# Gates of half the tokens through an accumulated table in DRAM

## The chip, the cores and the metric

The kernel runs on one core of a Trainium2 chip. A core has TensorE (matrix products into PSUM), VectorE, ScalarE and GpSimd (called POOL in the profile), SyncE, which here only issues DMAs, and 16 DMA engines that all queues share. The metric is the device time of one execution in microseconds; "span" is the part of it between the first and the last recorded instruction.

## The reference

A two-layer encoder for 256 tokens of width 1024. Layer 0 mixes tokens by a short gated convolution, layer 1 by windowed attention. After each mixer comes the part that this change is about, an expert layer with 8 heads (PEER). For each token and head it scores 128 + 128 sub-keys, takes the best 16 of each, adds them in pairs, keeps the best 16 of the sums as expert numbers out of 128 x 128, and weighs these with a softmax, the gates:

```python
top_v, pos = lax.top_k(cand, PEER_TOPK)
idx = jnp.take_along_axis(cidx, pos, axis=-1)
g = jax.nn.softmax(top_v, axis=-1)
...
h = jnp.einsum("cd,ced->ce", xc, u)
a = gc.astype(xc.dtype) * jax.nn.gelu(h, approximate=False)
return jnp.einsum("ce,ced->cd", a, jnp.take(v_tab, ic, axis=0))
```

So a token's output is a sum over its 128 selected experts. One expert can be selected by several heads of a token; its gates then add up.

## The kernel before

The kernel doesn't gather experts. It computes all 16384 of them for every token and multiplies by a dense matrix of gates that is zero where an expert was not selected. Everything is done in float32 split in two float32r parts, so each weight tile of 128 x 1024 is loaded by SyncE (`raw`), copied to `hi` by ScalarE (L171) and reduced to `lo` by VectorE (L172). `take()` hands out the tiles in a fixed order, loaded some tiles ahead.

One expert layer (`peer`, L597) runs in these stages, named by the PSUM tiles that TensorE writes:

- `pq` and `psc`: 16 query tiles and the scores of the sub-keys. The sub-keys (1 MB) come by a DMA on POOL's queue (L600).
- `ph`, twice 64 expert columns j (two halves): `hm[i, j, t]` is the GELU of token t with expert i*128 + j, where i is the partition. 64 KB per partition and half.
- `pv`: 128 rows j. `split_pair(j)` (L805) splits two rows of `hm` (ScalarE, then VectorE) into a ring that lies in the memory of `xn`, and twelve products of 512 columns per row accumulate into four banks.

The selection runs on VectorE beside these stages. `Background` (L35) holds a list of steps, each with a planned cost; every query tile, expert column and row calls `pump()`, which issues as many steps as the plan allows: `plan(cost, calls)` spreads `cost` over `calls`. The steps are `side` (best 16 of 128 sub-keys), `candidates`, `pick` (best 16 sums), `decode`, `lookup` and `total` (expert numbers), `gates` (softmax), `turned` (three products that put tokens on the free axis), and, ahead of ph, `normed`, which makes `xn`, the input of ph, out of `xr`.

When half 0 of ph is done, `one_hots` and `spread` build the dense gates of that half, eight tokens at a time: VectorE compares an iota with i (L754) and with j (L756), multiplies the second by three bfloat16 parts of the gate (L758), TensorE multiplies the two for each token (three products of 64 columns, PSUM tile `pg`), and VectorE multiplies the 128 x 64 result of eight tokens into `hm` (L770). These steps are spread over half 1 of ph; those of half 1 over the first rows of pv.

What sets the order: the engines each work in the order in which the program emits instructions for them, `tc.issue_after(x)` emits after x, and the framework adds waits for data and for buffers. POOL's queue carries, in this order, the write of the bias rows (L443) in the convolution, the sub-keys, the bias loads for attention (L449, L451) in the second half of pv of layer 0, the sub-keys of layer 1, and one load at the end (L858).

Of the kernel before, what the change touches and what calls it, by code (L numbers as in the profile page):

```python
# [17 lines left out]
P = 128  # L18
T = 256
# [11 lines left out]
NEG = -1e30  # L31
ROUTE, SPREAD, WARM = 88.0, 2.6, (9, 2, 2, 2, 4, 2)

# [38 lines left out]
def trunk_kernel(  # L72
# [77 lines left out]
    G.iota(iota2, pattern=[[1, P], [0, 2]], base=0, channel_multiplier=0, allow_small_or_imprecise_dtypes=True)  # L150
    i1T = const.tile([P, T], BF16, name="i1T")
    i2T = const.tile([P, T], BF16, name="i2T")
    gT = const.tile([P, 3, T], BF16, name="gT")
# [4 lines left out]
    zeros = const.tile([P, 512], BF16, name="zeros")  # L158
    V.memset(zeros, 0.0)
    S.activation(stat[:, 10:11], eps, AF.Square)  # L160
    squares = const.tile([P, 512], BF16, name="squares")

# [99 lines left out]

    def squares_of(t, h):
        return S.activation(
            squares, xs[:, t, 512 * h : 512 * h + 512], AF.Square, accum_out=stat[:, 2 * t + h : 2 * t + h + 1]
        ).ins
# [122 lines left out]
    def conv_mixer(sc):  # L389
# [35 lines left out]
        for k in range(KC - 2):  # L425
            rows_product(acc, take(), z[:, k, :T], z[:, k, T:], k == 0)
        return last_rows(acc, [(take(KC - k), z[:, k, :T], z[:, k, T:]) for k in (KC - 2, KC - 1)])


# [167 lines left out]
    def peer(layer, last, meanwhile):  # L597
# [44 lines left out]

        def candidates(t):
            s = sv[:, t].rearrange("p (h s) k -> p h s k", s=2)
            a, b = s[:, :, 0], s[:, :, 1]
            V.tensor_tensor(
                cand[:, :, 0:2].rearrange("p h r c -> p h (r c)"), b, a[:, :, 0:1].to_broadcast([P, PH, TOPK]), ALU.add
            )
            V.tensor_tensor(
                cand[:, :, 2:9],  # L650
                a[:, :, 1:8, None].to_broadcast([P, PH, 7, 8]),
                b[:, :, None, 0:8].to_broadcast([P, PH, 7, 8]),
                ALU.add,
            )
            V.tensor_tensor(cand[:, :, 9], a[:, :, 8:16], b[:, :, 0:1].to_broadcast([P, PH, 8]), ALU.add)
# [4 lines left out]
        def decode(t):  # L660
            flat = tp.rearrange("p h k -> p (h k)")
            V.tensor_scalar(line, flat, 3, None, op0=ALU.logical_shift_right)
            V.tensor_scalar(col, flat, 7, None, op0=ALU.bitwise_and)
            V.tensor_copy(linef, line)
            V.tensor_copy(colf, col)
            V.scalar_tensor_tensor(beyond, linef, 9.0, colf, op0=ALU.is_equal, op1=ALU.mult)
            V.tensor_tensor(colf, colf, beyond, ALU.subtract)
            V.scalar_tensor_tensor(ab[:, 0], linef, -1.0, beyond, op0=ALU.add, op1=ALU.add)
            V.tensor_scalar(ab[:, 0], ab[:, 0], 0.0, None, op0=ALU.max)
            V.tensor_scalar(linef, linef, 1.0, 8.0, op0=ALU.is_equal, op1=ALU.mult)  # L670
            V.tensor_tensor(ab[:, 1], linef, colf, ALU.add)

        def lookup(t, s):

            if s == 0:
                V.tensor_copy(sib, si[:, t, :, :, None].to_broadcast([P, NSUB, TOPK, 2]))
            V.tensor_tensor(
                pick16.rearrange("p a (k d) -> p a k d", d=2),
                ab[:, s, None, :].to_broadcast([P, TOPK, P]).rearrange("p a (k d) -> p a k d", d=2),
                iota16[:, :, None, :].to_broadcast([P, TOPK, P // 2, 2]),  # L680
                ALU.is_equal,
            )
            ids = sib.rearrange("p (h s) a d -> p s h a d", s=2)[:, s]
            for h in range(PH):
# [3 lines left out]
        def total(t, s):  # L688
            for n in (8, 4, 2):
                V.tensor_tensor(pick16[:, 0:n], pick16[:, 0:n], pick16[:, n : 2 * n], ALU.add)  # L690
            V.tensor_tensor(sel[:, s], pick16[:, 0], pick16[:, 1], ALU.add)

        def gates(t):
            g = sel[:, 2].rearrange("p (h k) -> p h k", h=PH)
            V.tensor_tensor(g, tv, tv[:, :, 0:1].to_broadcast([P, PH, TOPK]), ALU.subtract)
            S.activation(g, g, AF.Exp)
            V.tensor_reduce(small[:, 0], g, axis=AX.X, op=ALU.add)
            V.reciprocal(small[:, 1], small[:, 0])
            V.tensor_tensor(g, g, small[:, 1, :, None].to_broadcast([P, PH, TOPK]), ALU.mult)

        def turned(t):
# [3 lines left out]
            c = slice(P * t, P * t + P)  # L705
            S.copy(i1T[:, c], b[:, 0])
            S.copy(i2T[:, c], b[:, 1])
            r = beyond
            V.tensor_copy(gT[:, 0, c], b[:, 2])
            V.tensor_tensor(r, b[:, 2], gT[:, 0, c], ALU.subtract)  # L710
            V.tensor_copy(gT[:, 1, c], r)
            V.tensor_tensor(gT[:, 2, c], r, gT[:, 1, c], ALU.subtract)

        bg.plan(ROUTE, NSUB + HALF - 4)
        for c4 in range(0, NSUB, 4):
            q = qT[(c4 // 4) % 2]
            for c in range(c4, c4 + 4, 2):
                b = bank("u", "pq")
                for i in range(2):
                    cols_product(b[:, T * i : T * i + T], take(), xr, c + i)  # L720
                    bg.pump()
                S.copy(q[:, c - c4 : c - c4 + 2], b.rearrange("p (a t) -> p a t", a=2))
            if c4 == 0:
                factors()
                for k in range(0, KC, 2):
                    bg.add(2.2, normed, k)
# [7 lines left out]
        for t in range(NT):  # L734
            bg.add(0.9, candidates, t)
            for h in range(PH):
                bg.add(0.9, pick, t, h)
            bg.add(1.7, decode, t)
            for s in range(2):
                bg.add(3.4, lookup, t, s)  # L740
                bg.add(1.3, total, t, s)
            bg.add(0.7, gates, t)
            bg.add(0.6, turned, t)

# [15 lines left out]
        def spread(hm, t0, made):  # L760
            oh1, oh2 = made.pop(t0)
            b = bank("g", "pg").rearrange("p (t i) -> p t i", t=8)
            for t in range(8):
                for j in range(3):
# [3 lines left out]
                    )  # L768
            c = slice(t0, t0 + 8)
            V.tensor_tensor(hm[:, :, c], b.rearrange("p t i -> p i t"), hm[:, :, c], ALU.mult)  # L770
# [3 lines left out]
        for half in range(2):  # L774
# [28 lines left out]
        acc = accumulators("pv")  # L803

        def split_pair(j):  # L805
            a = aring[:, (j // 2) % 4]
            src = halves[j // HALF][:, j % HALF : j % HALF + 2].rearrange("p a t -> p (a t)")
            S.copy(a[:, 0], src)  # L808
            V.tensor_tensor(a[:, 1], src, a[:, 0].bitcast(F32), ALU.subtract)  # L809


        kept, held = (2, 3)[layer], []
        split_pair(0)
        for j in range(0, P, 2):
            if j == HALF - 2:
# [3 lines left out]
            if j + 2 < P:  # L819
                split_pair(j + 2)  # L820
            a = aring[:, (j // 2) % 4]
# [24 lines left out]

    last = peer(0, last, prepare_attention)
    last = attention(held.pop(), last)

# [123 lines left out]
```

## Time and profile before

| | |
|---|---|
| Median of 3 runs | 1840.79 us (1840.71 to 1844.92) |
| The profiled execution | 1841.05 us, span 1839.1 us |
| TensorE busy | 1821.1 us (99%), granted clock 0.999 |
| VectorE busy | 1459.1 us (79%) |
| ScalarE busy | 918.3 us (50%) |
| POOL busy | 10.8 us (1%), 20 instructions |
| Moved by DMA | 322.62 MB, mean 175 GB/s |

How to read the profile: a group of instructions stands on one line with its source line, engine, operation, the tile it writes and the tiles it reads, the shape, the count, then busy time in all and the mean of one in ns, then the idle time of the engine just before them and what ended it. The chain is the work that ended last, followed back from the end; in order of time its rows have start, duration and the instruction. In windows each engine has its busy time within a stretch.

### The profile page before, as it was taken

Reading aid. Unit: us, or ns where it says so; the run is one execution under the profiler, and the core shown is the slowest. Engines: PE = TensorE matmul, PEld = TensorE weight load, DVE = VectorE, ACT = ScalarE, POOL = GpSimd, SP = SyncE. Lnnn points to the kernel's source line nnn. Section 1 sums busy time; section 2 is a strip of 40 time slices with the busy share of each in tenths; the row PEclk is TensorE's granted clock in tenths of the full one; section 3 lists DMA queues with packets and bytes.
Section 4 is the critical chain, followed back from the end, with each engine's and each line's share of the span. In section 5 each row is a group of like instructions: output and inputs, shape, how many; then the busy total and the mean of one; then the engine's idle time right before and its main releaser. Section 6 shows DMA issues by size and latency. Waiting matters only on the chain.

```text
span 1839.1 us, 33102 instructions
## 1 busy us (share of the span) xinstructions
PE 1821.1 (99%) x13007; PEld 1598.9 (87%) x13007; DVE 1459.1 (79%) x2917; ACT 918.3 (50%) x1236; POOL 10.8 (1%) x20
## 2 busy tenths in 40 slices
PE   9999999999999999999999999999999999999998
PEld 7999999988888888888887999999888888888886
DVE  7868988688888898655575789877888899885555
ACT  5465455544454443444475655555445544444444
POOL 0000000000000001000000000000000000000000
PEclk9999999999999999999999999999999999999999
DMA  6654555555555556656643555555555555555553
GB/s 209 195 183 161 184 184 183 173 166 167 172 162 182 162 168 201 227 191 196 193 131 102 171 164 184 184 183 172 173 163 161 181 162 169 164 185 194 194 194 126
DMA packets 89047, 322.62 MB, mean 175 GB/s; under 512 B 10235, under 2 KB 10428, under 8 KB 88636
## 3 DMA queue, kind: packets, MB, share of 16 engines
q1 hardware_dynamic: 87120, 314.61, 53.7%
q0 software_dynamic: 1392, 5.81, 0.9%
q8 instruction: 101, 1.65, 0.4%
q14 instruction: 54, 0.44, 0.1%
q10 hardware_dynamic: 380, 0.10, 0.0%
HBM read 319.40 MB, written 1.08 MB: 174 GB/s over the span
## 4 chain that ended last, share of the span: by engine, by line
PE 96%; DVE 2%; ACT 1%; DMA 0%; issue 0%; ACTq 0%; DVEq 0%
PE ph L107 39%; PE pv L107 37%; PE pq L107 6%; PE pg L107 5%; PE pconv L107 2%; PE pwo L107 1%; PE psc L107 1%; PE pout L107 1%; PE pgate L107 1%; PE po L107 0%; DVE lo L172 0%; PE pk L107 0%; PE ptr L111 0%; PE pwarm L107 0%; DMA mix<-in_sink 0%; ACT xn L301 0%
## 5 line engine op out<-in xcount | busy, mean ns | idle before, releaser
L172 DVE TENSOR_TENSOR lo<-raw,hi 128x1024 fp32r<-128x1024 f32 (+1 forms) x597 | 726.2, 1219 | 257.0 <-ACT hi L171 142.7
L171 ACT CAST hi<-raw 128x1024 fp32r<-128x1024 f32 (+1 forms) x597 | 625.5, 1049 | 535.2 <-PE ph L107 214.3
L107 PE MATMUL ph<-xn,hi 128*128 128x512 f32 (+1 forms) x2592 | 515.8, 347 | 0.0
L107 PE MATMUL pv<-hi,xn 128*128 128x512 f32 x2048 | 509.2, 389 | 0.0
L107 PEld LDWEIGHTS pv<-hi,xn 128*128 128x128 f32 x2048 | 384.4, 188 | 81.1
L107 PEld LDWEIGHTS ph<-xn,hi 128*128 128x128 f32 x2592 | 403.2, 190 | 48.4
L107 PEld LDWEIGHTS ph<-xn,lo 128*128 128x128 f32 x2048 | 273.2, 191 | 16.0 <-DVE lo L172 1.3
L107 PE MATMUL ph<-xn,lo 128*128 128x256 f32 x2048 | 281.9, 283 | 0.9 <-DVE lo L172 0.9
L107 PE MATMUL pv<-lo,xn 128*128 128x512 f32 x1024 | 279.8, 393 | 0.4 <-DVE lo L172 0.4
L107 PEld LDWEIGHTS pv<-lo,xn 128*128 128x128 f32 x1024 | 189.6, 188 | 38.3 <-DVE lo L172 1.1
L808 ACT CAST xn<-hm 128x512 fp32r<-128x512 f32 x128 | 79.0, 623 | 190.2 <-PE pv L107 187.7
L758 DVE TENSOR_TENSOR oh<-oh,gT 128x512 bf16<-128x512 bf16 x384 | 139.1, 417 | 0.0
L809 DVE TENSOR_TENSOR xn<-hm,xn 128x512 fp32r<-128x512 f32 x128 | 87.6, 689 | 61.4 <-ACT xn L808 61.4
L107 PEld LDWEIGHTS <-oh 128*128 128x128 bf16 x3072 | 96.2, 97 | 9.7 <-issue 8.4
L107 PE MATMUL pg<-oh,oh 128*128 128x64 bf16 x3072 | 103.9, 193 | 0.0
L788 ACT ACTIVATE hm<-hm 128x512 f32<-128x512 f32 x94 | 59.4, 632 | 85.7 <-DVE hm L227 85.7
L754 DVE TENSOR_TENSOR oh<-iota,i1T 128x1024 bf16<-128x1024 bf16 x128 | 87.5, 684 | 12.0 <-PE pg L107 12.0
L770 DVE TENSOR_TENSOR hm<-pg,hm 128x512 f32<-128x512 f32 x128 | 87.3, 684 | 1.8 <-PE pg L107 1.7
L107 PE MATMUL pq<-xr,hi 128*128 128x256 f32 x512 | 68.7, 285 | 0.3
L107 PEld LDWEIGHTS pq<-xr,hi 128*128 128x128 f32 x512 | 64.4, 192 | 2.1 <-ACT xr L301 1.7
L227 DVE TENSOR_TENSOR hm<-ph,hm 128x512 f32<-128x512 f32 x94 | 64.1, 682 | 0.0
L226 ACT COPY hm<-ph 128x512 f32<-128x512 f32 x94 | 54.7, 582 | 0.0
(170 smaller groups left out, 1051.2 us busy)
## 6 DMA issues: line engine op xcount, KB each, us to landing
raw<-in_u SPq DMA_DIRECT2D x256, 512.0 KB, 3.6
raw<-in_v SPq DMA_DIRECT2D x256, 512.0 KB, 3.4
raw<-in_w_q SPq DMA_DIRECT2D x32, 512.0 KB, 3.4
raw<-in_w_in SPq DMA_DIRECT2D x23, 512.0 KB, 3.8
raw<-in_w_qk SPq DMA_DIRECT2D x10, 512.0 KB, 3.4
raw<-in_w_out SPq DMA_DIRECT2D x8, 512.0 KB, 3.4
raw<-in_w_o SPq DMA_DIRECT2D x8, 512.0 KB, 3.4
mix<-bias_dram POOLq DMA_DIRECT2D x8, 384.0 KB, 10.5
```

The costliest lines, as they stand in the source:

```text
L107: newest[:] = [PE.matmul(*a, **k).ins]
L171: S.copy(hi[:, c], raw[:, c])
L172: bg.behind = V.tensor_tensor(lo[:, c], raw[:, c], hi[:, c].bitcast(F32), ALU.subtract).ins
L226: S.copy(dst, b[:, :, T:])
L227: V.tensor_tensor(dst, b[:, :, :T], dst, ALU.add)
L754: V.tensor_tensor(oh1, iota2[:, None].to_broadcast([P, 4, P, 2]), pairs(i1T, P), ALU.is_equal)
L758: V.tensor_tensor(oh2[:, 1 + j], oh2[:, 0], pairs(gT[:, j], HALF), ALU.mult)
L770: V.tensor_tensor(hm[:, :, c], b.rearrange("p t i -> p i t"), hm[:, :, c], ALU.mult)
L788: S.activation(hm[:, j : j + 2], hm[:, j : j + 2], AF.Gelu)
L808: S.copy(a[:, 0], src)
L809: V.tensor_tensor(a[:, 1], src, a[:, 0].bitcast(F32), ALU.subtract)
```

## The change

For the first 128 tokens the dense gates are no longer made from one-hots. They are added up in a table in DRAM, `table[i, j*128 + t]`, 128 x 16384 float32 (8.4 MB):

- `blank_table(n)` writes zeros into it with eight 1 MB DMAs on POOL's queue, n of them in flight: in layer 0 in the third column of the convolution, in layer 1 ahead of attention.
- `sent` works out on VectorE, for each token (partition) and each of its 128 selections, the address (i*128 + j)*128 + t, and `scatter(h)` issues for each head 16 indirect DMAs with addition, one for each of the 16 selections, each with one address and one gate per partition. The first two DMAs of a head wait until all of the head before have landed, since two heads can name the same cell.
- In pv, `load_gates(j)` loads two rows' gates for all first tokens (128 partitions x 1 KB), in a ring of two buffers on POOL's queue, and `gated(j)` multiplies them into `hm` on VectorE ahead of `split_pair(j)`.
- The second 128 tokens go by one-hots as before; those steps, `i1T`, `i2T`, `gT` and the transposes are there for 128 tokens only.
- The selection steps take a range of heads. Of token half 0, heads 0 and 1 are done first, during the query tiles and ahead of `normed`; then heads 2 to 7 of it, then token half 1. Planned costs change; `normed` is emitted at the latest at the end of the query tiles.

```diff
-ROUTE, SPREAD, WARM = 88.0, 2.6, (9, 2, 2, 2, 4, 2)
+FIRST, SPREAD, WARM = 24.0, 2.6, (9, 2, 2, 2, 4, 2)
...
             if j == 2:
                 bias_rows(sc)
+                blank_table(1)
...
+    table = dram.tile([P, P * P], F32, name="table")
+    cells = table.rearrange("p (f o) -> (p f) o", o=1)
+    ROWS = 2048
...
+    def blank_table(n):
+
+        blanked[:] = [bg.behind] * n
+        for i in range(P * P // ROWS):
+            dst = table[:, ROWS * i : ROWS * i + ROWS].rearrange("p (a c) -> p a c", c=256)
+            ins = nc.gpsimd.dma_start(dst, blank[:, None, :].to_broadcast([P, ROWS // 256, 256])).ins
+            wait_for(ins, blanked[:1])
+            blanked[:] = blanked[1:] + [ins]
+
+    def scatter(h):
+
+        earlier = blanked[:] if h == 0 else group[:]
+        group.clear()
+        for k in range(TOPK):
+            c = slice(TOPK * h + k, TOPK * h + k + 1)
+
+            def one():
+                group.append(
+                    nc.gpsimd.indirect_dma_start(
+                        cells, bass.IndirectOffsetOnAxis(ap=place[:, c], axis=0), gate[:, c], None,
+                        compute_op=ALU.add,
+                    ).ins
+                )
+
+            if k < 2:
+                one()
+                wait_for(group[k], earlier)
+            else:
+                with tc.issue_after(group[0]):
+                    one()
+            for g in group[:-1]:
+                tc.declare_no_dep(group[-1], g, reason="other cells")
...
+        def sent(h0, h1):
+
+            c = slice(TOPK * h0, TOPK * h1)
+            V.scalar_tensor_tensor(linef[:, c], sel[:, 0, c], float(P), sel[:, 1, c], op0=ALU.mult, op1=ALU.add)
+            V.tensor_scalar(place[:, c], linef[:, c], float(P), token, op0=ALU.mult, op1=ALU.add)
+            for h in range(h0, h1):
+                scatter(h)
...
+        def routed(t, h0, h1):
+            n = (h1 - h0) / PH
+            bg.add(0.3 + 0.6 * n, candidates, t, h0, h1)
+            for h in range(h0, h1):
+                bg.add(1.0, pick, t, h)
+            bg.add(1.2 + 1.3 * n, decode, t, h0, h1)
+            for s in range(2):
+                bg.add(0.4 + 3.2 * n, lookup, t, s, h0, h1)
+                bg.add(0.5 + 0.9 * n, total, t, s, h0, h1)
+            bg.add(0.5 + 0.4 * n, gates, t, h0, h1)
+            if t == 0:
+                bg.add(0.4, sent, h0, h1)
+            else:
+                bg.add(1.0, turned)
...
-        bg.plan(ROUTE, NSUB + HALF - 4)
+        bg.plan(FIRST, NSUB)
...
-                for c in range(c4, c4 + 4):
-                    bg.add(1.0, side, t, c)
...
+            for c in range(c4, c4 + 4):
+                bg.add(1.4, side, 0, c)
+            if c4 == 0:
+                routed(0, 0, 2)
+                for k in range(0, KC, 2):
+                    bg.add(2.2, normed, k)
+                last_normed = bg.steps[-1]
+        while last_normed in bg.steps:
+            bg.step()
+        routed(0, 2, PH)
+        for c in range(NSUB):
+            bg.add(1.4, side, 1, c)
+        routed(1, 0, PH)
+        bg.plan(sum(step[0] for step in bg.steps), HALF - 4)
...
-            bg.plan(SPREAD * T // 8, HALF - 4)
+            bg.plan(SPREAD * P // 8, HALF - 4)
             made = {}
-            for t0 in range(0, T + 8, 8):
-                if t0 < T:
+            for t0 in range(0, P + 8, 8):
+                if t0 < P:
                     bg.add(SPREAD - 0.6, one_hots, half, t0, made)
...
+        ended = bg.behind
...
+        first, gates_of, sent_last = [], {}, group[:]
+
+        def load_gates(j):
+            g = strm.tile([P, 2, P], F32, tag="gates", name="gates", bufs=2)
+            load = lambda: nc.gpsimd.dma_start(g, table[:, P * j : P * j + 2 * P].rearrange("p (a t) -> p a t", a=2)).ins
+            if not first:
+                first.append(load())
+                wait_for(first[0], sent_last)
+            else:
+                with tc.issue_after(first[0]):
+                    load()
+            gates_of[j] = g
+
+        def gated(j, behind):
+            h = halves[j // HALF][:, j % HALF : j % HALF + 2, :P]
+            with tc.issue_after(behind):
+                return V.tensor_tensor(h, h, gates_of.pop(j), ALU.mult).ins
...
         kept, held = (2, 3)[layer], []
+        load_gates(0)
+        load_gates(2)
+        ins = gated(0, ended)
+        load_gates(4)
         split_pair(0)
+        gated(2, ins)
+        load_gates(6)
         for j in range(0, P, 2):
...
             if j + 2 < P:
-                split_pair(j + 2)
+                ins = split_pair(j + 2)
+            if j + 4 < P:
+                gated(j + 4, ins)
+            if j + 8 < P:
+                load_gates(j + 8)
...
     last = peer(0, last, prepare_attention)
+    blank_table(2)
     last = attention(held.pop(), last)
```

More of the change, by code (lines that the diff above doesn't have):

```diff
@@ L150, in trunk_kernel @@
     G.iota(iota2, pattern=[[1, P], [0, 2]], base=0, channel_multiplier=0, allow_small_or_imprecise_dtypes=True)
-    i1T = const.tile([P, T], BF16, name="i1T")
-    i2T = const.tile([P, T], BF16, name="i2T")
-    gT = const.tile([P, 3, T], BF16, name="gT")
+    token = const.tile([P, 1], F32, name="token")
+    G.iota(token, pattern=[[0, 1]], base=0, channel_multiplier=1, allow_small_or_imprecise_dtypes=True)
+    i1T = const.tile([P, P], BF16, name="i1T")
+    i2T = const.tile([P, P], BF16, name="i2T")
+    gT = const.tile([P, 3, P], BF16, name="gT")
+    place = const.tile([P, P], U32, name="place")
+    gate = const.tile([P, P], F32, name="gate")
     stat = const.tile([P, 16], F32, name="stat")
@@ L157, in trunk_kernel @@
     V.memset(eps, EPS * D)
-    zeros = const.tile([P, 512], BF16, name="zeros")
-    V.memset(zeros, 0.0)
+    blank = const.tile([P, 256], F32, name="blank")
+    V.memset(blank, 0.0)
+    zeros = blank.bitcast(BF16)
     S.activation(stat[:, 10:11], eps, AF.Square)
-    squares = const.tile([P, 512], BF16, name="squares")
     def split_tile(src, spare=False, pieces=1):
@@ L263, in squares_of @@
     def squares_of(t, h):
+        squares = strm.tile([P, 512], BF16, tag="gates", name="squares", bufs=2)
         return S.activation(
@@ L427, in conv_mixer, with wait_for @@
         return last_rows(acc, [(take(KC - k), z[:, k, :T], z[:, k, T:]) for k in (KC - 2, KC - 1)])
+    table = dram.tile([P, P * P], F32, name="table")
+    cells = table.rearrange("p (f o) -> (p f) o", o=1)
+    ROWS = 2048
+    blanked, group = [], []
+    def wait_for(ins, others):
+        for o in others:
+            tc.add_manual_dep(
+                ins, o.name, mybir.DependencyInfo(mybir.DependencyClass.Sync, mybir.DependencyReason.DATA),
+                reason="transfers of one table in turn",
+            )
[17 more added lines that the diff above has]
+                    ).ins
+                )
+            if k < 2:
[6 more added lines that the diff above has]
+                tc.declare_no_dep(group[-1], g, reason="other cells")
     bias_dram = dram.tile([HEADS, 511], F32, name="bias_dram")
@@ L639, in side, with candidates @@
             best16(sv[:, t, c], si[:, t, c], scores[:, t, c], rest[turn[0] % 4])
-        def candidates(t):
-            s = sv[:, t].rearrange("p (h s) k -> p h s k", s=2)
+        def candidates(t, h0, h1):
+            n = h1 - h0
+            s = sv[:, t, 2 * h0 : 2 * h1].rearrange("p (h s) k -> p h s k", s=2)
             a, b = s[:, :, 0], s[:, :, 1]
+            to = cand[:, h0:h1]
             V.tensor_tensor(
-                cand[:, :, 0:2].rearrange("p h r c -> p h (r c)"), b, a[:, :, 0:1].to_broadcast([P, PH, TOPK]), ALU.add
+                to[:, :, 0:2].rearrange("p h r c -> p h (r c)"), b, a[:, :, 0:1].to_broadcast([P, n, TOPK]), ALU.add
@@ L648, in candidates @@
             )
             V.tensor_tensor(
-                cand[:, :, 2:9],
-                a[:, :, 1:8, None].to_broadcast([P, PH, 7, 8]),
-                b[:, :, None, 0:8].to_broadcast([P, PH, 7, 8]),
+                to[:, :, 2:9],
+                a[:, :, 1:8, None].to_broadcast([P, n, 7, 8]),
+                b[:, :, None, 0:8].to_broadcast([P, n, 7, 8]),
                 ALU.add,
             )
-            V.tensor_tensor(cand[:, :, 9], a[:, :, 8:16], b[:, :, 0:1].to_broadcast([P, PH, 8]), ALU.add)
+            V.tensor_tensor(to[:, :, 9], a[:, :, 8:16], b[:, :, 0:1].to_broadcast([P, n, 8]), ALU.add)
@@ L657, in pick @@
         def pick(t, h):
             best16(tv[:, h], tp[:, h], cand[:, h].rearrange("p r c -> p (r c)"), crest[h % 2])
[L660 to L671, printed above, removed]
@@ L673, in lookup, with decode @@
-        def lookup(t, s):
+        def decode(t, h0, h1):
+            c = slice(TOPK * h0, TOPK * h1)
+            flat = tp[:, h0:h1].rearrange("p h k -> p (h k)")
+            r, o, rf, of, by = (a[:, c] for a in (line, col, linef, colf, beyond))
+            V.tensor_scalar(r, flat, 3, None, op0=ALU.logical_shift_right)
+            V.tensor_scalar(o, flat, 7, None, op0=ALU.bitwise_and)
+            V.tensor_copy(rf, r)
+            V.tensor_copy(of, o)
+            V.scalar_tensor_tensor(by, rf, 9.0, of, op0=ALU.is_equal, op1=ALU.mult)
+            V.tensor_tensor(of, of, by, ALU.subtract)
+            V.scalar_tensor_tensor(ab[:, 0, c], rf, -1.0, by, op0=ALU.add, op1=ALU.add)
+            V.tensor_scalar(ab[:, 0, c], ab[:, 0, c], 0.0, None, op0=ALU.max)
+            V.tensor_scalar(rf, rf, 1.0, 8.0, op0=ALU.is_equal, op1=ALU.mult)
+            V.tensor_tensor(ab[:, 1, c], rf, of, ALU.add)
@@ L675, in lookup @@
+        def lookup(t, s, h0, h1):
+            n, c = TOPK * (h1 - h0), slice(TOPK * h0, TOPK * h1)
             if s == 0:
-                V.tensor_copy(sib, si[:, t, :, :, None].to_broadcast([P, NSUB, TOPK, 2]))
+                V.tensor_copy(
+                    sib[:, 2 * h0 : 2 * h1], si[:, t, 2 * h0 : 2 * h1, :, None].to_broadcast([P, 2 * (h1 - h0), TOPK, 2])
+                )
             V.tensor_tensor(
-                pick16.rearrange("p a (k d) -> p a k d", d=2),
-                ab[:, s, None, :].to_broadcast([P, TOPK, P]).rearrange("p a (k d) -> p a k d", d=2),
@@ L680, in lookup @@
-                iota16[:, :, None, :].to_broadcast([P, TOPK, P // 2, 2]),
+                pick16[:, :, c].rearrange("p a (k d) -> p a k d", d=2),
+                ab[:, s, None, c].to_broadcast([P, TOPK, n]).rearrange("p a (k d) -> p a k d", d=2),
+                iota16[:, :, None, :].to_broadcast([P, TOPK, n // 2, 2]),
                 ALU.is_equal,
@@ L683, in lookup, with total, gates, turned @@
             ids = sib.rearrange("p (h s) a d -> p s h a d", s=2)[:, s]
-            for h in range(PH):
+            for h in range(h0, h1):
                 e = pick16[:, :, TOPK * h : TOPK * h + TOPK].rearrange("p a (k d) -> p a k d", d=2)
                 V.tensor_tensor(e, e, ids[:, h, :, None, :].to_broadcast([P, TOPK, TOPK // 2, 2]), ALU.mult)
-        def total(t, s):
+        def total(t, s, h0, h1):
+            c = slice(TOPK * h0, TOPK * h1)
             for n in (8, 4, 2):
[L690 to L695, printed above, removed]
-            S.activation(g, g, AF.Exp)
[L697 to L701, printed above, removed]
+                V.tensor_tensor(pick16[:, 0:n, c], pick16[:, 0:n, c], pick16[:, n : 2 * n, c], ALU.add)
+            V.tensor_tensor(sel[:, s, c], pick16[:, 0, c], pick16[:, 1, c], ALU.add)
+        def gates(t, h0, h1):
+            n = h1 - h0
+            g = (sel[:, 2] if t else gate).rearrange("p (h k) -> p h k", h=PH)[:, h0:h1]
+            v = tv[:, h0:h1]
+            V.tensor_tensor(g, v, v[:, :, 0:1].to_broadcast([P, n, TOPK]), ALU.subtract)
+            S.activation(g, g, AF.Exp)
+            V.tensor_reduce(small[:, 0, h0:h1], g, axis=AX.X, op=ALU.add)
+            V.reciprocal(small[:, 1, h0:h1], small[:, 0, h0:h1])
+            V.tensor_tensor(g, g, small[:, 1, h0:h1, None].to_broadcast([P, n, TOPK]), ALU.mult)
+        def sent(h0, h1):
+            c = slice(TOPK * h0, TOPK * h1)
+            V.scalar_tensor_tensor(linef[:, c], sel[:, 0, c], float(P), sel[:, 1, c], op0=ALU.mult, op1=ALU.add)
+            V.tensor_scalar(place[:, c], linef[:, c], float(P), token, op0=ALU.mult, op1=ALU.add)
+            for h in range(h0, h1):
+                scatter(h)
+        def turned():
             b = bank("g", "psel").rearrange("p (s q) -> p s q", s=4)
@@ L704, in turned @@
                 transpose(b[:, s], sel[:, s], ident)
-            c = slice(P * t, P * t + P)
-            S.copy(i1T[:, c], b[:, 0])
-            S.copy(i2T[:, c], b[:, 1])
+            S.copy(i1T, b[:, 0])
+            S.copy(i2T, b[:, 1])
             r = beyond
[L709 to L712, printed above, removed]
-        bg.plan(ROUTE, NSUB + HALF - 4)
+            V.tensor_copy(gT[:, 0], b[:, 2])
+            V.tensor_tensor(r, b[:, 2], gT[:, 0], ALU.subtract)
+            V.tensor_copy(gT[:, 1], r)
+            V.tensor_tensor(gT[:, 2], r, gT[:, 1], ALU.subtract)
+        def routed(t, h0, h1):
+            n = (h1 - h0) / PH
+            bg.add(0.3 + 0.6 * n, candidates, t, h0, h1)
+            for h in range(h0, h1):
+                bg.add(1.0, pick, t, h)
[9 more added lines that the diff above has]
+        bg.plan(FIRST, NSUB)
         for c4 in range(0, NSUB, 4):
@@ L724, in peer @@
                 factors()
-                for k in range(0, KC, 2):
-                    bg.add(2.2, normed, k)
             for t in range(NT):
@@ L731, in peer @@
                 S.activation(scores[:, t, c4 : c4 + 4], b, AF.Copy, scale=stat[:, 8 + t : 9 + t])
-                for c in range(c4, c4 + 4):
-                    bg.add(1.0, side, t, c)
[L734 to L743, printed above, removed]
+            for c in range(c4, c4 + 4):
[12 more added lines that the diff above has]
+        bg.plan(sum(step[0] for step in bg.steps), HALF - 4)
         def one_hots(half, t0, made):
@@ L768, in spread @@
                     )
-            c = slice(t0, t0 + 8)
+            c = slice(P + t0, P + t0 + 8)
             V.tensor_tensor(hm[:, :, c], b.rearrange("p t i -> p i t"), hm[:, :, c], ALU.mult)
```

2 lines of the change are left out of this document (1 added, 1 removed).

## The prediction

> **What bounds the kernel now.** I read the page first: busy times, granted clock, chain.
>
> ```profile
> PE 1821.1 (99%) x13007; PEld 1598.9 (87%) x13007; DVE 1459.1 (79%) x2917; ACT 918.3 (50%) x1236; POOL 10.8 (1%) x20
> PEclk9999999999999999999999999999999999999999
> PE 96%; DVE 2%; ACT 1%; DMA 0%; issue 0%; ACTq 0%; DVEq 0%
> q1 hardware_dynamic: 87120, 314.61, 53.7%
> ```
>
> TensorE sets the end everywhere, at full clock. POOL, which the change uses, is idle. Then the chain in order of time, layer 0:
>
> ```profile
> 105.67 11.70 PE pq L107 x92
> ...
> 157.86 1.83 PE psc L107 x16
> 159.69 110.66 PE ph L107 x784
> ...
> 356.56 1.47 PE pg L107 x48
> 358.03 11.24 PE ph L107 x64
> ...
> 546.17 13.63 PE pv L107 x60
> 559.80 1.47 PE pg L107 x48
> 561.27 11.01 PE pv L107 x48
> ```
>
> The one-hot products (pg) stand in the chain as 1.47 us blocks, 48 products for 16 tokens, between blocks of ph (2.81 us per expert column: 64 products are four) and of pv (2.75 us per row: 48 are four). So half 0 is spread while half 1 of ph runs, and half 1 during the first rows of pv. Third, the groups:
>
> ```profile
> L107 PE MATMUL pg<-oh,oh 128*128 128x64 bf16 x3072 | 103.9, 193 | 0.0
> L758 DVE TENSOR_TENSOR oh<-oh,gT 128x512 bf16<-128x512 bf16 x384 | 139.1, 417 | 0.0
> L754 DVE TENSOR_TENSOR oh<-iota,i1T 128x1024 bf16<-128x1024 bf16 x128 | 87.5, 684 | 12.0 <-PE pg L107 12.0
> L756 DVE TENSOR_TENSOR oh<-iota,i2T 128x512 bf16<-128x512 bf16 x128 | 53.5, 418 | 0.0
> L770 DVE TENSOR_TENSOR hm<-pg,hm 128x512 f32<-128x512 f32 x128 | 87.3, 684 | 1.8 <-PE pg L107 1.7
> L416 DVE TENSOR_TENSOR mix<-mix 128x256 f32<-128x256 f32 x8 | 3.4, 424 | 0.2
> ```
>
> And the stages, by windows:
>
> ```profile
> core 0: us, PE busy (x) PEld busy (x) DVE busy (x) ACT busy (x) POOL busy (x), PEclk, DMA share, GB/s
> 20.00:80.00 60.00, 59.88 (x407) 54.57 (x406) 53.67 (x89) 27.06 (x35) 0.67 (x1) 1.00 0.60 189
> 105.00:160.00 55.00, 54.89 (x455) 54.28 (x454) 41.84 (x105) 32.73 (x52) 0.00 (x0) 1.00 0.56 179
> 160.00:270.00 110.00, 110.00 (x781) 103.64 (x780) 102.02 (x358) 59.00 (x72) 0.00 (x0) 1.00 0.57 182
> 270.00:340.00 70.00, 69.55 (x491) 65.26 (x491) 53.09 (x144) 39.52 (x51) 0.00 (x0) 1.00 0.59 183
> 546.00:703.00 157.00, 157.00 (x1228) 130.63 (x1227) 141.94 (x235) 67.86 (x79) 0.00 (x0) 1.00 0.55 170
> 720.00:745.00 25.00, 24.64 (x191) 20.18 (x190) 20.22 (x35) 10.60 (x12) 6.30 (x9) 1.00 0.85 296
> 745.00:905.00 160.00, 160.00 (x708) 132.48 (x707) 92.27 (x88) 76.96 (x88) 0.00 (x0) 1.00 0.60 194
> ```
>
> VectorE is near its limit only in the routing (102 of 110 us). From 720 to 745 us the bias loads raise the DMA share to 0.85 and TensorE still works 24.64 of 25 us: DMA has that much room.
>
> **The change, part by part.**
>
> *Removed from TensorE.* 3072/48 = 64 blocks of 1.47 us = 94 us, all on the path; half of the tokens is half of them: **-47 us**. With them go the turning of token half 0 (three products per layer, under 1 us, left out), and on VectorE half of 139.1 + 87.5 + 53.5 + 87.3 us, that is 184 us, off the path.
>
> *Added on VectorE in pv.* One product per pair of rows, 256 elements: 424 ns by L416, 128 of them, 54 us. One group of eight tokens costs VectorE 367.4/128 = 2.87 us; some 25 of the 128 groups fall between 546 and 703 us, so it loses about 36 us there and gains 28 times 0.42 = 12; after 745 us it goes from 92 to 105 of 160 us. Covered by TensorE.
>
> *Routing on VectorE.* Small instructions follow each other at 0.13 us, as two of the decoding show in order of time:
>
> ```profile
> 290.43 0.22 DVE L662 TENSOR_SCALAR route<-route 128x128 uint32<-128x128 uint32 x1
> 290.56 0.22 DVE L663 TENSOR_SCALAR route<-route 128x128 uint32<-128x128 uint32 x1
> ```
>
> The steps of token half 0 come in two groups (heads 0-1, 2-7): about 28 more small instructions and four for the addresses, less four around the turning: +3 to +4 us per layer. From 270 to 340 us VectorE has 17 us idle, and the plan ends there as before, so 0; without that cover 4 us per layer. The sharper edge is xn: before, it was ready early.
>
> ```profile
> L628 DVE TENSOR_TENSOR xn<-route,xn x4: 684/685/685, 121.8 to 138.2; 128x512 fp32r<-128x512 f32 x4
> ```
>
> Now four sides (5.6 planned us) and heads 0-1 (8.8) go ahead of it; at 24 planned us over the 12 pumps that are left, the last of the four is issued with the last pq, near 157 us, and ph wants it at 159.7. Lateness 0 to 6 us per layer (four such steps are 8 us of VectorE, less the psc block); I take 2, so **+4 us**.
>
> *Blanking.* 8.4 MB per layer in eight 1 MB writes on POOL's queue. In layer 0 they start behind the bias row's write (31 us), one at a time, beside weights at share 0.60.
>
> ```profile
> bias_dram<-mix POOLq DMA_DIRECT2D x1, 31.9 KB, 3.1
> route<-in_subk POOLq DMA_DIRECT2D x2, 1024.0 KB, 5.1
> last<-in_last_gain POOLq DMA_DIRECT2D x1, 512.0 KB, 7.5
> mix<-bias_dram POOLq DMA_DIRECT2D x8, 384.0 KB, 10.5
> ```
>
> 1 MB takes 5.1 us in a quiet place, perhaps 9 here, so they end between 72 and 103 us. Queued behind them on POOL is the load of the subkeys, issued at 103.8 us and first used by psc at 118.04: it fits, cost 0; at 12 us a write the load is late by 14 us. In layer 1 two are in flight from about 905 us, and the subkeys go at 1014.7: 0.
>
> *The scatter.* Per layer 8 heads times 16 DMAs of 128 four-byte additions, 128 issues on POOL; each head also waits for the one before. Heads 0-1 can go at about 148 us, the rest when 34.9 of 80.6 planned us are done, 26 of 60 pumps of 2.81 us after 159.7: 233 us. The first gates are wanted when pv starts, 546 - 8 x 1.47 = 534 us, and a load before that lands in some 7 us, so the scatter has to end by 527. Eight waits at 3.5 us (a small write landed in 3.1) leave (527 - 148 - 28)/128 = **2.74 us per DMA**. No indirect DMA stands in this trace. Nearest rows, POOL in order of time:
>
> ```profile
> 0.28 0.10 POOL L963 MEMSET const-float32-1.0<- 128x1 f32 x1
> 0.31 0.10 POOL L963 MEMSET const-bfloat16-1.0<- 128x1 bf16 x1
> ...
> 103.80 0.55 POOL L600 DMA_DIRECT2D route<-in_subk  x1 [72.24 <-PE pout L107]
> ...
> 723.20 0.54 POOL L449 DMA_DIRECT2D mix<-in_sink  x1 [618.84 <-DVE xn L809]
> 723.73 5.77 POOL L451 DMA_DIRECT2D mix<-bias_dram  x8
> ```
>
> From below: 0.72 us, a direct DMA of 256 rows (0.54 for 128). From above: each index handled alone at the closest spacing of two POOL instructions, 35 ns, 128 x 0.035 = 4.5 us. I take 1.4 us, twice the direct one, nearest to the rows that are DMAs: done near 233 + 96 x 1.4 + 6 x 3.5 = 388 us. Cost 0.
>
> *What the scatter does to the weights.* Each of 16 engines gets 1024 additions a layer. Small packets in the first 60 us:
>
> ```profile
> q10 hardware_dynamic: 380, 0.10, 0.8%
> ```
>
> 0.8% of 16 x 60 us over 380 packets is 20 ns each; from above, an addition as long as a weight packet, 53.7% of 16 x 1839.1 us over 87120 = 181 ns. I take 60 (read, read, write): 61 us over 379, share 0.56 + 0.16, under the 0.85 that did no harm. Cost 0; at 181 ns 208 + 185 us of engine work stand against 379: 15 us per layer.
>
> *Gate loads.* 64 of 128 KB per layer, in a ring of two: issued when the product two pairs earlier frees the buffer, due two pairs (10.9 us) later. Behind a waiting product on VectorE stand the weights' low parts and the next split, and TensorE behind those. By the rows above they land in 3 to 7.5 us, hidden. Behind a bias load (layer 0, eight times) up to 14 us: 0 to 3 us each, at most 25; I take 0, since the bias loads now go out one per four rows instead of at once.
>
> **Sum.** Against the profiled execution, 1841.05 us (span 1839.1; 0.3 above the median of 1840.79): 1841 - 47 + 4 = **1798 us**.
>
> **Rivals.**
>
> *A, POOL cannot keep up.* Above 2.74 us per DMA the scatter ends after pv wants it, and TensorE waits at the start of pv in both layers; above about 2.9 us the change loses. At 4.5 us: 128 x 4.5 + 28 - 379 = 225 us per layer, 1798 + 450 = 2248 us. For it: 128 separate indices. Against it: 256 rows of a direct DMA cost only 0.18 us more than 128. [...]
>
> *B, the additions hold the DMA engines.* At 181 ns: 1798 + 2 x 15 = 1828 us; from 188 ns on nothing of the gain is left. [...] Against: 20 ns packets. [...]
>
> *C, late gates.* With one load per pair and two buffers, a landing over 10.9 us makes every pair wait. At the 14.2 us that the slowest bias load took (below) a pair takes 7.3 instead of 5.4 us: 1.9 x 62 x 2, 2034 us. For it: 1 KB rows 64 KB apart. Against: 512 KB landed in 7.5 us.
>
> ```profile
> DMA to landing us min/median/max: 7.0/10.5/14.2
> ```
>
> *D, covers go one by one.* xn late (12 us in all), the subkeys (14), the routing (8), the loads behind bias (25): up to 59, which is no change; half of it is 1824.
>
> **How the numbers follow.** Forecast 68%, with its own range 1791 to 1815; B 8%; D 7%, most of it within the band; C 7%; A 10%. A measurement here tells 0.3%, 5.5 us, from no change. Faster: forecast, B and a light C, 77%; the same: D, 6%; slower: A, most of C and an end of D, 17%. The range, 1790 to 1842, holds the forecast, B and most of D and leaves out A and C.
>
> **What would show it.** pg x1536 in 32 blocks of 1.47 us, ph and pv blocks as long as now. POOL: 256 indirect issues under 2.7 us each, the last in layer 0 landed well before 520 us; no idle TensorE near 534 us and no VectorE wait on the gates. xn's last part against the first ph tells the +4. Weight landings under 7 us during the scatter speak against B; gate landings under 10 us against C. The forecast is wrong if a pv block stands behind a POOL or DMA release, or if the blocks of ph grow while the scatter runs.

## The result, and the profile after

The changed kernel takes 1794.55 us in the median (1793.74 to 1795.58), the kernel before 1840.75 us (1840.59 to 1844.92): a ratio of 0.9744, interval 0.9727 to 0.9761. The forecast was 1798 us. The profiled execution of after took 1794.28 us with a span of 1792.5 us; that of before, 1841.05 and 1839.1.

First the page of after: busy times, the two DMA queues that matter, the costliest groups, and DMA issues (KB each, median us to landing).

```profile
PE 1770.9 (99%) x11462; PEld 1552.5 (87%) x11465; DVE 1351.8 (75%) x2717; ACT 917.2 (51%) x1234; POOL 608.1 (34%) x421
...
q1 hardware_dynamic: 87120, 314.61, 56.6%
q0 software_dynamic: 48752, 39.52, 12.0%
...
L467 POOL DMA_INDIRECT table<-gate,place x256 | 513.9, 2007 | 235.6 <-issue 105.9
...
L910 DVE TENSOR_TENSOR hm<-hm,gates 128x256 f32<-128x256 f32 x128 | 53.7, 421 | 2.9 <-DMA gates<-table 2.9
...
table<-blank POOLq DMA_DIRECT2D x16, 1024.0 KB, 7.7
...
gates<-table POOLq DMA_DIRECT2D x128, 128.0 KB, 4.3
```

TensorE still fills 99% of the span; it has 50 us less to do. POOL went from 1% to 34% busy, 514 of its 608 us in the 256 indirect DMAs, 2.0 us each. The groups of the one-hots in after:

```profile
L107 PE MATMUL pg<-oh,oh 128*128 128x64 bf16 x1536 | 52.0, 193 | 0.0
L841 DVE TENSOR_TENSOR oh<-iota,i1T 128x1024 bf16<-128x1024 bf16 x64 | 44.0, 687 | 8.6 <-PE pg L107 8.6
L857 DVE TENSOR_TENSOR hm<-pg,hm 128x512 f32<-128x512 f32 x64 | 43.9, 686 | 1.4 <-PE pg L107 1.3
```

They are half of what they were, with means within 3 ns. In the chain of waits they stand as before, in blocks of 48 products (layer 1; start, us, what):

```profile
1257.10 1.47 PE pg L107 x48
1258.57 22.41 PE ph L107 x128
```

Windows of after, for the zeros (27 to 91 us), the larger part of the scatter of layer 0 (235 to 483) and the same stretch of pv as before:

```profile
core 0: us, PE busy (x) PEld busy (x) DVE busy (x) ACT busy (x) POOL busy (x), PEclk, DMA share, GB/s
27.00:91.00 64.00, 64.00 (x416) 57.89 (x415) 55.58 (x88) 27.80 (x35) 7.87 (x9) 1.00 0.95 320
235.00:483.00 248.00, 248.00 (x1752) 224.67 (x1751) 192.77 (x421) 132.99 (x168) 198.95 (x97) 1.00 0.73 181
546.00:703.00 157.00, 157.00 (x981) 130.37 (x980) 125.02 (x190) 71.14 (x82) 19.59 (x35) 1.00 0.67 207
```

In none of the three does TensorE wait, not even where the zeros raise the DMA share to 0.95. VectorE has 125 us of work in pv where it had 142.

Where the time went is seen by cutting the span at the first convolution product, the first query product after each mixer, the first ph, the first pv, and the first pk. The lengths in us, of every kernel whose stages the text speaks of ("mixer" is convolution or attention):

| | mixer 0 | pq, psc 0 | ph 0 | pv 0 | mixer 1 | pq, psc 1 | ph 1 | pv 1 and end |
|---|---|---|---|---|---|---|---|---|
| before | 93.8 | 55.1 | 386.6 | 376.4 | 92.9 | 55.1 | 386.5 | 382.2 |
| after | 94.4 | 56.4 | 373.6 | 363.0 | 95.2 | 56.4 | 373.6 | 369.5 |
| products twice | 94.4 | 56.4 | 385.3 | 374.6 | 95.2 | 56.4 | 385.3 | 381.1 |
| one-hots twice | 94.4 | 56.4 | 376.1 | 371.6 | 95.8 | 56.4 | 376.4 | 375.4 |
| one-hots twice, apart | 94.5 | 56.4 | 375.7 | 370.0 | 95.9 | 56.4 | 376.1 | 375.2 |
| squares apart | 93.8 | 55.1 | 373.6 | 363.0 | 92.9 | 55.1 | 373.6 | 369.5 |

From before to after the four stages of ph and pv lose 13.0 + 13.4 + 12.9 + 12.7 = 52.0 us, and the other four grow by 0.6 + 1.3 + 2.3 + 1.3, which is 5.6 before rounding: net 46.4. The rest of the spans' difference (46.6) lies ahead of the first convolution product. So the total is near the 43 us that the prediction took off, and its parts aren't: five microseconds more were won and five were lost where nothing was expected.

### The profile page after: what moved, and what is told of

Its sections match the earlier page's. It is cut to its first block, busy times and chain, and to the rows that moved or that the text cites. A ratio compares the mean times of both kernels' runs of the same rounds, so it can differ in the third digit from the quotient of the medians.

```text
span 1792.5 us, 30471 instructions
## 1 busy us (share of the span) xinstructions
PE 1770.9 (99%) x11462; PEld 1552.5 (87%) x11465; DVE 1351.8 (75%) x2717; ACT 917.2 (51%) x1234; POOL 608.1 (34%) x421
## 5 line engine op out<-in xcount | busy, mean ns | idle before, releaser
L177 DVE TENSOR_TENSOR lo<-raw,hi 128x1024 fp32r<-128x1024 f32 (+1 forms) x597 | 728.0, 1221 | 297.0 <-ACT hi L176 144.2
L467 POOL DMA_INDIRECT table<-gate,place x256 | 513.9, 2007 | 235.6 <-issue 105.9
L898 POOL DMA_DIRECT2D gates<-table x128 | 69.1, 540 | 675.8 <-DVE hm L910 622.4
L845 DVE TENSOR_TENSOR oh<-oh,gT 128x512 bf16<-128x512 bf16 x192 | 69.8, 421 | 0.1
L454 POOL DMA_DIRECT2D table<-blank x16 | 14.4, 903 | 125.1 <-DMA table<-blank 57.7
L910 DVE TENSOR_TENSOR hm<-hm,gates 128x256 f32<-128x256 f32 x128 | 53.7, 421 | 2.9 <-DMA gates<-table 2.9
```

The source lines that it names most:

```text
L177: bg.behind = V.tensor_tensor(lo[:, c], raw[:, c], hi[:, c].bitcast(F32), ALU.subtract).ins
L467: nc.gpsimd.indirect_dma_start(cells, bass.IndirectOffsetOnAxis(ap=place[:, c], axis=0), gate[:, c], None, compute_op=ALU.add,).ins
L845: V.tensor_tensor(oh2[:, 1 + j], oh2[:, 0], pairs(gT[:, j], HALF), ALU.mult)
L898: load = lambda: nc.gpsimd.dma_start(g, table[:, P * j : P * j + 2 * P].rearrange("p (a t) -> p a t", a=2)).ins
L910: return V.tensor_tensor(h, h, gates_of.pop(j), ALU.mult).ins
```

## The loss in the other stages

What TensorE waited for, in all (us in total, times, longest), first before, then after:

```profile
PE pconv L107 <- ACT hi L171: 1.4, 1, 1.4
...
PE ph L107 <- DVE lo L172: 0.9, 2, 0.5
PE pq L107 <- ACT mix L532: 0.7, 1, 0.7
PE pv L107 <- DVE lo L172: 0.4, 1, 0.4
```

```profile
PE pq L107 <- ACT hi L176: 2.2, 2, 1.1
PE pconv L107 <- ACT hi L176: 2.1, 2, 1.4
PE pq L107 <- ACT mix L585: 1.6, 1, 1.6
...
PE pk L107 <- ACT hi L176: 1.1, 1, 1.1
```

Waits on VectorE's `lo` are gone; new or longer are waits on `hi`, ScalarE's copy of a weight tile, in each stage that follows a norm. ScalarE in order of time at the first of them, before and after, and TensorE in after:

```profile
106.26 0.65 ACT L264 ACTIVATE squares<-xs 128x512 bf16<-128x512 f32 x1
...
106.88 1.06 ACT L171 CAST hi<-raw 128x1024 fp32r<-128x1024 f32 x1
107.82 0.64 ACT L264 ACTIVATE squares<-xs 128x512 bf16<-128x512 f32 x1
```

```profile
108.51 0.63 ACT L270 ACTIVATE squares<-xs 128x512 bf16<-128x512 f32 x1
...
109.12 2.94 ACT L176 CAST hi<-raw 128x1024 fp32r<-128x1024 f32 x3
```

```profile
110.22 2.17 PE L107 MATMUL pq<-xr,hi 128*128 128x256 f32 x16 [1.08 <-ACT hi L176]
```

Before, squares for the norm and weight copies took turns. In after all four squares go first (106.67 to 109.12 us), and three copies stand behind them. The line of the diff that does this has nothing to do with gates: the unused result of the squares, which had one tile of its own, was moved into the ring of two buffers named `gates`. The excerpt of the diff above doesn't show that line, and the prediction didn't cost it at all.

## The experiments

**1. The products twice.** Is the gain TensorE's time in the products, or something that came with their removal?

```diff
-                for j in range(3):
+                for j in (0, 1, 2) * 2:
```

> Every one-hot product of the second 128 tokens is made twice (the second pass writes the same sums into the same bank), so TensorE gets back as many products as the change removed, while VectorE keeps its lighter load. Theory T (the gain is the 32 removed blocks of 1.47 us on TensorE and nothing else): 1794.6 + 47 = 1841 us, pg x3072 in the trace, VectorE busy as in the changed kernel (about 1352 us). Rival V (the gain comes from the 107 us taken off VectorE, and TensorE only followed): 1795 to 1800 us.

1840.94 us (ratio to before 1.0, 0.9991 to 1.0009). The chain has the blocks at 96 products:

```profile
1280.34 2.92 PE pg L107 x96
```

32 blocks longer by 1.45 us are 46.4 us, and the time rose by 46.4. The products are on the path and hidden by nothing, at the price of the prediction. That the time comes out at that of before is a coincidence: by the table, ph and pv are 5.4 us shorter than before and the other stages 5.6 us longer.

**2. No table.** Leaves out the zeros, the scatter, the loads and the multiplications, so the first 128 tokens get no gates.

```diff
-        blanked[:] = [bg.behind] * n
+        return
...
-            for h in range(h0, h1):
-                scatter(h)
...
         def load_gates(j):
+            return
...
         def gated(j, behind):
+            return behind
```

> All work on the table is left out: no zeros, no indirect additions, no loads of gates and no products with them; the first 128 tokens stay without gates, which changes the output. What is left is the changed kernel without its new DMAs and without 54 us of VectorE. Theory T (all of that is hidden): 1793 to 1795 us. Rival H (the table costs several us on the path, made up elsewhere): 1785 to 1790 us.

1793.68 us (0.9739, 0.9724 to 0.9754), 0.9 us less than after, and by the intervals not to be told from it. The stages have the difference in mixer 1 (94.3 against 95.2 us), where the zeros of layer 1 are written; ph and pv keep their lengths to 0.1 us. All the new work together costs TensorE next to nothing: the zeros, 256 indirect DMAs, 128 loads and 54 us of VectorE lie beside it but for that.

**3. One head more, two heads more.** How far is the scatter from the edge? The last head is sent again, with zeros in place of gates (16 more indirect DMAs each time; the diff is of the first kernel, the second has `range(2)`).

```diff
+            if h1 == PH:
+                for _ in range(1):
+                    scatter(PH - 1, nothing=True)
```

> After head 7 the scatter adds one more group of 16 indirect DMAs, with zeros to head 7's cells, so it ends later by 16 x 2.31 + 4 = 41 us per layer; nothing else changes. In the changed kernel the loads of the first gates go out at 483 us, land 4 to 5 us later and are used at 532, so 44 us are free. Theory T (a fixed end is all that counts): it just fits, 1794.5 to 1797 us, with first gates landing some 3 us before their use. Rival (any longer scatter costs, by its load on the DMA engines): 1797 to 1810 us.

1794.56 us (0.9749, 0.9733 to 0.9765): no cost. The first gates are loaded at 526.3 us and the scatter was done just before; POOL in order of time:

```profile
518.79 2.56 POOL L467 DMA_INDIRECT table<-blank,place  x1 [0.30 <-issue]
526.30 1.20 POOL L901 DMA_DIRECT2D gates<-table  x2 [4.96 <-ACT hm L878]
```

> Two such groups: the scatter ends 82 us later, 38 us past its end in each layer. Theory T: TensorE waits for the first gates at the start of pv, 2 x 38 = 76 us more, 1870 us (1860 to 1880). Rival L (the first product can slip, since other work fills in for it): under 1815 us.

1856.45 us (1849.08 to 1858.05; ratio 1.0075, 1.0051 to 1.0099), slower than before by 0.75%. What TensorE waited for, and that wait in layer 0:

```profile
PE pv L107 <- ACT xn L918: 55.7, 2, 28.4
```

```profile
563.85 1.65 PE L107 MATMUL pv<-lo,xn 128*128 128x512 f32 x3 [28.38 <-ACT xn L918]
```

The profile names ScalarE's split, but that waits for VectorE's product, which waits for gates, which wait for the scatter: rival A, at its place and with its sign. It takes two heads more per layer. The size was off: 28 us per layer came, not 38, in the main because POOL got faster once the others stood still, and the last group took 30.5 us where the one before it took 37.9 (POOL in order of time, then a window with the columns as above):

```profile
504.49 2.54 POOL L467 DMA_INDIRECT table<-blank,place  x1 [0.30 <-issue]
...
531.22 1.54 POOL L467 DMA_INDIRECT table<-blank,place  x1 [0.30 <-issue]
```

```profile
528.00:556.00 28.00, 7.47 (x98) 7.24 (x96) 4.20 (x5) 2.53 (x4) 23.43 (x16) 0.69 0.40 55
```

The waits are 55.7 of the 61.9 us that this kernel is above the one with one head more. Pv after the stall is 2.7 and 2.9 us longer (365.7 and 372.4 us against 363.0 and 369.5), which makes 61.3; the granted clock fell to 0.69 in the window shown and stood at 0.85 from 556 to 600 us.

**4. The one-hots twice.** The prediction called VectorE covered. Here the five instructions that build a group's one-hots are issued twice, TensorE's products once.

```diff
+            for _ in range(2):
+                V.tensor_tensor(oh1, iota2[:, None].to_broadcast([P, 4, P, 2]), pairs(i1T, P), ALU.is_equal)
...
+                for j in range(3):
+                    V.tensor_tensor(oh2[:, 1 + j], oh2[:, 0], pairs(gT[:, j], HALF), ALU.mult)
```

> The five VectorE instructions that build the one-hots of eight tokens are issued twice, 64 groups of 2.19 us, about 140 us more on VectorE; TensorE's products stay as in the changed kernel. Theory T: VectorE has room in these stages, 1794.6 to 1797 us. Rival V: a good part of the gain goes, 1815 us or more.

1815.38 us (0.9858, 0.9843 to 0.9873): 21 us lost. The theory behind the prediction missed; VectorE counts. Since the second building stood in the same step as the first, the bunching might have done it, so a further kernel makes it a step of its own, with the plan's cost halved.

```diff
-                    bg.add(SPREAD - 0.6, one_hots, half, t0, made)
+                    bg.add((SPREAD - 0.6) / 2, one_hots, half, t0, made)
+                    bg.add((SPREAD - 0.6) / 2, one_hots, half, t0, made)
```

> As the run with the one-hots built twice, but the second building is a step of its own with half of the planned cost each, so VectorE's extra 140 us come in pieces of 2.2 us at even distances instead of 4.4 us at a time. Theory R (VectorE has room for the old load, and the 21 us that the first of these runs lost came from the bunching): 1794 to 1800 us. Theory V2 (the load itself is too much: with 150 of 160 us busy at the start of pv, VectorE is the bound there): 1808 to 1817 us.

1812.68 us (0.9841, 0.9825 to 0.9858). Spacing gave back under 3 us; it is the load. The spaced kernel's page, what its TensorE waited for, and a window of its pv:

```profile
PE 1781.8 (98%) x11465; PEld 1551.5 (86%) x11465; DVE 1467.0 (81%) x3037; ACT 921.2 (51%) x1234; POOL 625.9 (35%) x421
```

```profile
PE pv L107 <- DVE lo L177: 7.4, 11, 1.7
```

```profile
540.00:700.00 160.00, 157.38 (x944) 128.53 (x944) 151.26 (x263) 71.57 (x82) 15.10 (x28) 1.00 0.64 198
```

VectorE has 151 of 160 us of work here and delivers the weights' low parts late. Of the loss only 7.4 us are idle time of TensorE; the rest shows as longer busy time (1781.8 against 1770.9 us), and the one-hot products, busy for 55.7 us in place of 52.0, come in an estimated 54 pieces in place of 32 blocks (48 of them show 1.63 us in one block, one alone 0.193). VectorE's busy total, 1467 us, is close to the 1459 us of before (in layer 0, ph 326 us against 334 and pv 288 against 280). So a change that had halved the products and left VectorE its old amount of work would have kept some 28 of the 46 us; that is an estimate, since no run does just this.

**5. `xn` first.** The prediction charged 4 us for the late `xn`. Here `normed` goes ahead of heads 0 and 1.

```diff
-                routed(0, 0, 2)
                 for k in range(0, KC, 2):
                     bg.add(2.2, normed, k)
                 last_normed = bg.steps[-1]
+                routed(0, 0, 2)
```

> The four steps that make xn go ahead of heads 0 and 1 of the first tokens again, as in the kernel before; heads 0 and 1 reach the scatter some 10 to 14 us later. The prediction's +4 us (xn late at the start of ph) would come back: 1790.5 us. By the trace of the changed kernel xn's last part is done at 160.3 us and TensorE starts ph at 161.2 without a wait: 1794 to 1795.5 us.

1795.86 us (0.9755, 0.9738 to 0.9771): nothing gained, so there was nothing to gain.

**6. The squares apart.** They get one tile again, in memory shared with `place` and `gate`, which are not in use at those times.

```diff
-    place = const.tile([P, P], U32, name="place")
-    gate = const.tile([P, P], F32, name="gate")
+    shared = const.tile([P, 2 * P], F32, name="shared")
+    place, gate = shared[:, :P].bitcast(U32), shared[:, P:]
...
-        squares = strm.tile([P, 512], BF16, tag="gates", name="squares", bufs=2)
         return S.activation(
-            squares, xs[:, t, 512 * h : 512 * h + 512], AF.Square, accum_out=stat[:, 2 * t + h : 2 * t + h + 1]
+            shared.bitcast(BF16), xs[:, t, 512 * h : 512 * h + 512], AF.Square, accum_out=stat[:, 2 * t + h : 2 * t + h + 1]
```

> The output of the squares for the norm goes to one tile again, which shares the memory of the addresses and gates of the scatter, instead of the ring of two that it shares with the gate loads. ScalarE's order is then one square, one weight copy in turn, as in the kernel before, not four squares ahead of the copies. Theory S (the 1.1 us that TensorE waits for ScalarE's copy early in pq of each layer comes from that order): 1.5 to 3 us less than the changed kernel, 1791.6 to 1793 us. Rival (the copy is late because of the sub-keys' load or the zeros): 1794 to 1795 us.

1789.78 us (1788.27 to 1790.07; ratio 0.9719, 0.9706 to 0.9733), 4.8 us under after: more than expected, since time came back in all four stages ahead of ph (table above) and not only in pq. The stages are those of the profiled execution, which at 1788.27 us was the fastest of the five. What TensorE still waits for:

```profile
PE po L107 <- ACT mix L584: 4.8, 7, 0.7
...
PE pconv L107 <- ACT hi L176: 1.0, 1, 1.0
PE pq L107 <- ACT mix L584: 0.7, 1, 0.7
```

The stages ahead of ph have their old lengths to 0.1 us, ph and pv keep the gain. Its interval and that of after overlap a little (0.9727 to 0.9733), but its slowest run is 3.7 us under the fastest of after, and the trace shows the waits that went. This is the fastest of the kernels, ahead of both before and after.

## Why the prediction came out, point by point

**-47 for the products: right, and a little low.** The products alone are 46.4 us by experiment 1. But a block also slows the four products behind it. TensorE in order of time, the four behind a block of pv and the next four of the same kind, in before and in after:

```profile
561.11 1.17 PE L107 MATMUL pv<-lo,xn 128*128 128x512 f32 x4
...
563.95 1.07 PE L107 MATMUL pv<-lo,xn 128*128 128x512 f32 x4
```

```profile
560.78 1.17 PE L107 MATMUL pv<-lo,xn 128*128 128x512 f32 x4
...
563.63 1.07 PE L107 MATMUL pv<-lo,xn 128*128 128x512 f32 x4
```

The first four take 0.10 us longer, the same under the heavy load of VectorE in before and the lighter one in after. Over all blocks it is 0.09 us behind a block of ph and 0.10 behind one of pv, so the 32 blocks that went took another 3.1 us with them. The prediction's 1.47 us, read off the chain, leaves that out, and experiment 1 can't show it, since it doubles the products within the 32 blocks that are left.

**VectorE off the path: near as a size, incomplete as a reason.** "Covered by TensorE" holds for the 54 us that were added (experiment 2). What went from VectorE is seen at TensorE as the 1.3 us of waits on `lo` shown above, which are gone. With the 3.1 us behind the blocks, and 0.5 us of other products within ph that went with the turning of half the tokens, that is 4.9 of the 5.4 us by which ph and pv are shorter than the products explain; the last 0.5 us were not traced. But the room on VectorE is narrow: experiment 4 adds 114 us to its busy time, in the stages from which one-hots had gone, and loses 18 to 21 us. So the relief was worth little by itself, and by the estimate of experiment 4 it is what let the gain in the products come in full. The prediction has it as neither.

**+4 for `xn`: wrong, it is 0.** In after, VectorE and then TensorE in order of time:

```profile
159.64 0.69 DVE L681 TENSOR_TENSOR xn<-route,xn 128x512 fp32r<-128x512 f32 x1
```

```profile
161.19 1.08 PE L107 MATMUL ph<-xn,lo 128*128 128x256 f32 x7
```

The last part ended at 160.33 us, 0.86 us before ph began, and ph waited for nothing. That ph began 1.7 us later than in before is the squares' doing; yet they gave no cover here, since `xn` is issued by the query tiles' pace and moved with them: with the squares apart it ended at 157.90 us and ph began at 158.77. Experiment 5 moved `xn` forward and gained nothing. The step that failed is the placing of the last part inside 0 to 6 us of lateness: the bounds held, and the value taken, 2 per layer, should have been their lower end.

**Not in the sum: +5.6 for the squares.** Of this, 0.9 us in mixer 1 needed the zeros of layer 1 as well (next point). By the medians the change took off 46.2 us: 46.4 for the products and 5.4 beside them, less 5.6. The sum -47 + 4 said 43. That it came within 4 us is partly luck: two misses of more than 5 us each have opposite signs and cancel.

**Blanking at 0: right in layer 0, 0.9 us in layer 1.** The eight writes of layer 0 were issued from 27.75 to 82.72 us, landing in 7.7 us in the median of both layers (9 were assumed), and the window above shows TensorE without a wait at a DMA share of 0.95, beyond the 0.85 that the argument had as its best evidence. In layer 1 the zeros go out from 890 to 921 us. From 885 to 960 us the weights `in_w_qk` land in 8.0 us in the median, against 4.2 in the kernel without the table, and ScalarE waits for three of them:

```profile
ACT hi L176 <- DMA raw<-in_w_qk: 8.6, 3, 3.5
```

TensorE's wait on `mix` in pq is 1.6 us in after and 0.7 without the table, which is the 0.9 us of experiment 2. With the squares apart and the zeros in place that wait is 0.7 us too and mixer 1 has the length of before, so the zeros cost something only where the weight copies were late already.

**The scatter at 0: right, its price too low.** POOL of after, in order of time: the first issue, the first of heads 2 to 7, the last of layer 0, and the first two gate loads.

```profile
144.47 1.85 POOL L467 DMA_INDIRECT table<-gate,place  x1 [39.71 <-DVE place L768]
...
235.00 2.29 POOL L467 DMA_INDIRECT table<-gate,place  x1 [19.57 <-DVE gate L762]
...
477.36 2.43 POOL L467 DMA_INDIRECT table<-gate,place  x1 [0.30 <-issue]
482.90 1.20 POOL L898 DMA_DIRECT2D gates<-table  x2 [3.11 <-ACT hi L176]
```

Heads 0 and 1 started at 144 us (148 predicted), the rest at 235 (233). One DMA took 2.01 us and 0.30 until the next, 2.31 instead of 1.4, so the last issue ended at 480 us, not 388. The bound of 2.74 us, worked out from both ends, is what carried the forecast, and experiment 3 confirms its kind: 40 us more per layer fit, 80 don't. By that bound a DMA dearer by a fifth (0.43 us on 2.31) would have brought rival A about, which is closer than its 10% suggests.

**The additions at 60 ns: 42.** The DMA view of after from 235 to 480 us (packets, MB, share of 16 engines; then median us to landing):

```profile
q1 hardware_dynamic: 12081, 43.98, 59.2%
q0 software_dynamic: 13680, 0.05, 13.2%
...
raw<-in_u SPq DMA_DIRECT2D x84, 512.0 KB, 3.7
```

13.2% of 16 x 245 us over 13680 packets is 38 ns. 1520 of them, 16 for each DMA, are short (7 ns in the mean), which leaves 42 ns for each of the 12160 additions. Weights still land in 3.7 us. Rival B needed 181. That an addition is made of a read, a read and a write, from which the 60 came, no run shows; the runs show 42 ns in all.

**Late gates (C): no.** Landings of the gate loads in after:

```profile
DMA to landing us min/median/max: 2.4/4.3/10.2
```

The longest, 10.2 us, is under the two pairs' 10.9; VectorE waited 2.9 us for gates in all (page above), and TensorE never. **The covers of D: all held.** The stall that did come, the squares', was not on its list, since that line is none of the parts that the prediction took the change to have.

## What to carry to other kernels

When work leaves an engine that is 79% busy and feeds the one that sets the end, that relief can be what lets the gain come: put the work back alone and measure, before calling it covered. When a kind of product goes from between others, look at the products behind it too: here 32 blocks fewer were worth 3.1 us more than their own length. For an operation that the trace doesn't show, work out the price at which it would begin to hurt; here the bound of 2.74 us held while the guessed price was off by two thirds. And read every line of a diff for the order that it changes: moving an unused result into another ring cost 5 us of the gain, and was the cheapest thing to mend.

## What the runs showed of the hardware

An indirect DMA of 128 additions took POOL between 1.53 and 2.76 us to issue, and the short and the long ones came with different work beside them. In the stall of experiment 3, with VectorE busy 4.2 of 28 us, nearly every one took 1.54 us; with VectorE at work many took 2.4 to 2.6. In after, instructions of VectorE that read two tensors (TENSOR_TENSOR; the weights' low parts, L177, are the costliest) cover 49% of the time of the 60 shortest and 68% of that of the 60 longest; L177 itself was not slower (1221 ns against 1219 before). The DMA traffic was also lower in the stall (share 0.40 against 0.73), but in after it was much the same beside the 60 shortest (0.80) and the 60 longest (0.77). So by these shares VectorE is the likelier cause; no run changed it alone. For the prediction it means that a late scatter catches up in part: with the others waiting for it, the last group of experiment 3 took 30.5 us where the one before it took 37.9.
